# Two extra 512-column bf16 products in each step of three attentions, written into the PSUM ring's next bank

## The chip, the cores and the metric

The kernel runs on one core of one Trainium2 chip. The metric is the device time of one execution in microseconds (us). The kernel before was timed three times: 2797.93, 2802.47 and 2806.33 us, median 2802.47 us. The engines are called as in the profile: PE is TensorE (matrix products; PEld its weight loads), DVE VectorE, ACT ScalarE, POOL GpSimd, SP the engine that issues DMAs. PSUM is the memory that PE writes its products to, in eight banks of 512 fp32 columns.

## The reference

The program is four transformer layers on 256 tokens of width 1024, fp32 throughout. The first block has a gated MLP mixer and a differential attention, each followed by a squared-ReLU MLP and a gated input. The second block has two more attentions (`nsa_mixer`, `fox_mixer`), each followed by a mixture over 16384 small experts. Only the three attentions matter here. Cut to their cores:

```python
# differential attention: 8 heads, two score sets per head
sc = einsum('bqhcd,bkhcd->bhcqk', q, k) * scale            # causal, head dim 64
pr = softmax(sc);  attn = pr[:, :, 0] - lam * pr[:, :, 1]
o  = _rmsnorm(einsum('bhqk,bkhe->bqhe', attn, v), subln_g) * (1 - lambda_init)

# nsa: 16 heads, compressed keys plus two branches that here both see all causal keys
o = gate0 * (p_c @ v_cmp) + gate1 * (p_s @ v_slc) + gate2 * (p_w @ v_win)

# fox: 16 heads, scores with a running sum of forget gates
s = einsum('bhqd,bhkd->bhqk', q, k) + c[..., None] - c[:, :, None, :]
o = masked_softmax(s) @ v
```

## The kernel before

The 256 tokens are two tiles of 128 (tile 0, tile 1). Weights stream from HBM in blocks and each block is split into a high and a low float32r part (ACT makes the first, DVE the second); a product of two split numbers is three matmuls (`mm3`, lines 255 to 258). Four PSUM banks are the accumulators `A` (two per tile), the other four are a ring of scratch banks `B`: `ps` (line 260) takes the bank at the ring's front and puts it at the back. During an attention the ring is only two banks, since the other two hold the outputs.

An attention is written as a loop over units, one generator per tile (`unit(t)` in `diff_attention`, `nsa`, `fox`). A step of `attend` (line 899) issues up to seven parts, each of another unit, as a string says: `s` the scores (matmuls of 64 rows, 128 or 256 columns, then a bf16 mask product), `m` their row maxima on DVE, `e` the exponentials on ACT, `c` the scale, `t` the transposes on PE into a ring bank and the first part of their split on ACT, `l` the second part on DVE, `p` the products with v. With `"da": "t3l3c2p4e1s0m0"` a step turns the unit three back, and so on. A loop over n units has n plus the largest lag steps, so 12 steps per tile in the differential attention (da), 21 in nsa, 12 in fox; the last ones have no scores.

The order of the steps is a string too (`FILL`, read by `weave`): 0 and 1 are a step of tile 0's or tile 1's unit, c is a step of the product before the attention (six products of 512 columns), w one of the product after it. The program's order is the order on each engine's queue; nothing is rescheduled later. `identb` is a 128x128 bf16 identity, until now used only in the mask products (lines 1064, 1506, 1723).

```python
b = self.ring.pop(0)
self.ring.append(b)
```

Of the kernel before, what the change touches and what calls it, by code (L numbers as in the profile page):

```python
# [54 lines left out]
        "fox": "0cc0cc0c0c0c0111010101011010011w1w1w1w"}  # L55
ASIDE = {"go": "0234567", "wo": "0234567", "w10": "03", "w11": "", "nwo": "034567", "fwo": "0123457"}
# [3 lines left out]
def ffn_ops():  # L60
    """The pairs of up blocks ("u") and the down blocks ("d") in their order."""
    ops = [("u", 4)] + [("d", f) for f in range(4)] + [("u", 5)] + [("d", f) for f in range(4, 8)]
    for k in range(6, 14):
        ops += [("u", k), ("d", 2 * k - 4), ("d", 2 * k - 3)]
    return ops + [("u", 14), ("u", 15)] + [("d", f) for f in range(24, 32)]
# [5 lines left out]
class Stream:  # L71
    """The weights, block by block: a load, then the two float32r parts in a slot."""
# [9 lines left out]
    def aside(self, key):  # L82
        """True for the blocks whose second part GpSimd makes."""
        name, c = key[:-1], key[-1]
        while isinstance(name, tuple):
            name = "".join(str(x) for x in name) if not isinstance(name[0], tuple) else name[0]
        return str(c) in ASIDE.get(name, "")

# [3 lines left out]
    def open(self, pool, n):  # L92
        """n more slots, for the blocks that the plan lets use them."""
        self.free += [self._slot(pool, self.k.nm("x"), True) for _ in range(n)]
# [18 lines left out]
    def _one(self):  # L113
        """Splits the next block, if there is room for it."""
# [56 lines left out]
class Wide:  # L171
    """[128, 1024] in two banks of PSUM, of which one can be written while the other is read."""
# [15 lines left out]
class Build:  # L188
# [17 lines left out]
    def tick(self):  # L206
        """One step of each task."""
# [14 lines left out]
    def begin(self, task):  # L222
        """A task whose first step goes out at once."""
        next(task, None)
        return self.add(task)
# [4 lines left out]
    def need(self, t):  # L230
        """The input of a stage, tile t."""
# [28 lines left out]
    def ps(self, shape):  # L260
        """The next bank of the ring, as a shape."""
# [22 lines left out]
    def rstd(self, ms, eps, table=True, beside=None, r=None):  # L284
        """(ms + eps) ** -0.5, by ScalarE's table or, to leave its tables alone, by GpSimd; ms may be in two parts.

        beside() goes out while it is on its way."""
# [20 lines left out]
    def load_table(self, func):  # L308
        """ScalarE's table of func, ahead of its use."""
# [12 lines left out]
    def transpose_split(self, src, dst, c0, n, tsl, scale=None):  # L322
        """src [128 tokens, n*128]: chunks c0.. of dst[hi/lo][:, c, tsl]."""
# [8 lines left out]
    def wait(self, n):  # L332
        """Steps in which weights aren't split."""
# [5 lines left out]
    def turn_raw(self, t, xt, wait):  # L339
        """h's tile t, transposed and split into xt, without the norm's gain (the weights have it) and its r."""  # L340
# [6 lines left out]
    def turn_normed(self, t, g, xt, wait, table, part):  # L347
        """rmsnorm of h's tile t, transposed and split into xt; the last norm without xt."""
# [11 lines left out]
    def chain(self, t, m, post, pre, xt, wait=5, table=True):  # L360
        """h += m, or its rmsnorm; then the next stage's norm, with its gain pre or raw."""
# [25 lines left out]
    def block(self, key, c, x, t, out, ws, ncols, start, stop):  # L387
        """out[:, n] (tokens of tile t) += x^T w over row chunk c."""
# [13 lines left out]
    def ahead(self, keys, x, after=None, ncols=1024, start=True, stop=True):  # L402
        """Steps of a product for tile 0; those for tile 1 are put off."""
# [14 lines left out]
    def late(self):  # L418
        """The next block put off; False without one."""
# [18 lines left out]
    def linear(self, keys, x, after=None, ncols=1024, start=True, stop=True, lag=LAG, func=None):  # L438
        """A product for both tiles, tile 1 LAG blocks behind; after(t) once tile t is done.

        Towards the end tile 1 falls up to lag blocks behind, to be done beside what follows for tile 0, and func's
        table is loaded."""
# [13 lines left out]
    def lin_b(self, key, x, out):  # L456
        """out [n, tokens] of one block [128, 8, n]."""
# [134 lines left out]
    def open_side(self, n_gain):  # L592
        """What all but the expert layers use besides: a second input, slots of the stream, gains."""
# [7 lines left out]
    def dump(self, stage):  # L601
        """Ends the program after a stage, for tests of a part."""
# [42 lines left out]
    def load_x(self):  # L645
        """The input, the first weights before and between its tiles."""
# [4 lines left out]
    def load_p(self, i, also=None):  # L651
        """The layer's p, transposed, in two parts."""
# [8 lines left out]
    def proj(self, i, c, t, pt, ws):  # L661
        """pp = p w_proj, row chunk c of tile t."""
# [6 lines left out]
    def gmlp(self, xt, yt):  # L669
        nc, tc, a = self.nc, self.tc, self.a  # L670
        with tc.tile_pool(name="gm", bufs=1) as gp:
# [55 lines left out]
            def spatial():  # L727
                """s + b of all groups; u s of tile 0."""
# [46 lines left out]
    def ffn(self, i, xr, xt, also=None):  # L775
        """xr holds the raw input, xt will hold the normed one, xr the next stage's."""
# [72 lines left out]
    def scaled(self, x, t):  # L849
        """x = A[t] times the norm's r."""  # L850
# [3 lines left out]
    def inverse(self, t):  # L854
        """1 / r as a row."""
# [8 lines left out]
    def ple(self, i, xt, nxt):  # L864
# [11 lines left out]
        def mid(t, c):  # L876
            """The bias over r, that the sigmoid's scale takes back."""
# [21 lines left out]
    def attend(self, n, order, **parts):  # L899
        """Steps over n units: each one's parts trail one another, as far as order says.  # L900

        s: the scores; m: their maxima; e: the exponentials; c: the scale; t: the transposes and their first part;
        l: the second one; p: the product with v."""
        order = [(parts[k], int(b)) for k, b in zip(order[::2], order[1::2])]
        for i in range(n + max(b for _, b in order)):
            for f, b in order:
                if 0 <= i - b < n:
                    f(i - b)
            yield

    def weave(self, order, units, join, make):
        """The steps of both tiles' units (0, 1), those of tile 1's product before (c) and of tile 0's after (w).

        join(t) ends what tile t's units need, before the first of them or where order has z (0) or u (1); make begins
        the product after."""
# [39 lines left out]
    def maxima(self, s, n):  # L955
        """The negated row maxima of the score sets s [128, n, kn]."""
# [4 lines left out]
    def exps(self, s, n, kn, e, nm):  # L961
        """e = exp of the score sets s [128, n, kn] plus nm; the rows' sums."""
# [5 lines left out]
    def low(self, parts):  # L968
        """The second part of what the first was copied from."""
# [7 lines left out]
    def normed(self, e, r, kn, engine):  # L977
        """e [128, 2, kn] times r [128, 2]."""
# [17 lines left out]
    def diff_attention(self, xt, vx):  # L996
        """vx holds v and, after its use, nothing; xt becomes the input of w_o."""
        nc, tc, a = self.nc, self.tc, self.a
        H = 8
        with tc.tile_pool(name="da", bufs=1) as gp, tc.tile_pool(name="daw", bufs=2) as wp:  # L1000
# [48 lines left out]
            def unit(t):  # L1049
                """Steps of one component of two heads each."""  # L1050
# [25 lines left out]
                def scale(i):  # L1076
                    """e0 - lam (sum0 / sum1) e1; the rows' 1 / sum0 are left to fin."""
# [42 lines left out]
                return self.attend(H, ORDER["da"], s=scores, m=peak, e=soft, c=scale, t=turn, l=low, p=pv)  # L1120

            def fin(t, q, p3, norm):
                """The rmsnorm of four heads' norm p3."""
# [27 lines left out]
    def prep_rotary(self, pool):  # L1151
        """Steps to cos and sin of positions * inv_freq, [128, 2 tiles, 8], and lambda."""
# [62 lines left out]
    def rope64(self, dst, src, t, nh, wp, v=None):  # L1215
        """dst, src [128, nh, 64]; by VectorE or v."""
# [14 lines left out]
    def nsa(self):  # L1231
        """Tokens are fewer than the window and than the selected blocks: both branches see all keys."""
        nc, tc, a = self.nc, self.tc, self.a
        xt, qT = self.xb, self.xa
        with ExitStack() as ctx:
# [8 lines left out]
            # the compressed values of group g in rows 32j, at j, g; zeros in the other rows  # L1244
# [23 lines left out]
            def dup(x, fn, wait):  # L1268
                """x [128, 4, 2, 64] -> psum [128 = 2 copies of 64, 4, 128 tokens]; fn(p)."""
# [27 lines left out]
            def four(t):  # L1297
                """k and v of the compressed branch, k and v of the selected one."""
# [23 lines left out]
            def two(t):  # L1322
                """k and v of the window; the gates."""
# [14 lines left out]
            def build(kv):  # L1338
                """The blocks of tokens, with their places' embeddings."""
# [46 lines left out]
            def tail():  # L1386
                """The compressed keys and values."""
# [67 lines left out]
            def compressed(t):  # L1455
                """The compressed branch's weights of all heads, [128, 16, 32] with 16 used.

                Head (g, r) is at 8 (g // 2) + 4 (r // 2) + 2 (g % 2) + r % 2."""
# [32 lines left out]
            def unit(t):  # L1491
# [34 lines left out]
                def turn_compressed(a):  # L1526
                    """The weights of heads 8a.., turned."""
# [25 lines left out]
                def pv(i):  # L1553
# [7 lines left out]
                    def add(y, stop):  # L1561
                        """The compressed branch of a pair."""
# [19 lines left out]
                return self.attend(16, ORDER["nsa"], s=scores, m=peak, e=soft, c=scale, t=turn, l=low, p=pv)  # L1582
# [9 lines left out]
    def fox(self):  # L1592
# [3 lines left out]
        with ExitStack() as ctx:  # L1596
# [10 lines left out]
            # rows (1, 1, c_hi, c_lo) for queries and (-c_hi, -c_lo, 1, 1) for keys, of head 8a + 4v + 2u + w at  # L1607
            # 32 (2v + w), 2a + u: those that share a bank of scores are in the same rows
# [21 lines left out]
            def forget():  # L1630
                """c, the running sums of the forget gates' logarithms, into cx."""
# [73 lines left out]
            def unit(t):  # L1705
# [60 lines left out]
                return self.attend(8, ORDER["fox"], s=scores, m=peak, e=soft, c=scale, t=turn, l=low, p=pv)  # L1766
# [8 lines left out]
    def peer(self, li, side):  # L1775
        """All experts' products, times the gates (0 where an expert isn't chosen)."""
# [3 lines left out]
        with ExitStack() as ctx:  # L1780
# [20 lines left out]
            def select():  # L1801
                for t in range(NT):
# [24 lines left out]
                    # softmax over the 16 best  # L1827
# [15 lines left out]
                    # the entries of topi at the positions, by one-hot rows  # L1843
# [83 lines left out]
            def gbuild(half):  # L1927
                """H[half] *= G: the gates by expert (i, j) and token, from one-hot rows by selection."""
# [45 lines left out]
            def spread(bg, done, i, n, steps):  # L1974
                """bg's steps so far, after block i of n."""
# [40 lines left out]
            def weights(upto):  # L2016
                """The halves' rows, times the gates, in the input's place."""
# [37 lines left out]
def layout(inputs):  # L2055
    """The arrays of the program: the inputs laid out, and constants of the shapes."""
# [72 lines left out]
```

## Time and profile before

| what | value |
|---|---|
| median of three runs | 2802.47 us (2797.93 to 2806.33) |
| profiled execution, first to last instruction | 2807.0 us |
| PE busy | 2721.5 us, 97% |
| DVE, ACT, POOL busy | 2043.0, 1337.9, 141.0 us |
| mean granted TensorE clock | 0.964 of full |

The profiled execution is a run of its own. Its span, 2807.0 us, is already 0.7 us above the slowest of the timed runs, and what lies around the span is not in the profile. The page cuts the span into 40 slices of 70.2 us; the line PEclk gives the clock that was granted in each. A timeline row gives start, duration, engine, line and operation of one instruction; the difference of two starts is the pace. Matmuls overlap, so a pace is shorter than a duration.

### The profile page before, as it was taken

To read this page: it belongs to the slowest core of one execution; us is meant where nothing else is said; L and a number is where in the kernel's file an instruction comes from. 1 tells how busy PE (TensorE), PEld (TensorE's weight loads), DVE (VectorE), ACT (ScalarE), POOL (GpSimd) and SP (SyncE) were. 2 spreads that over 40 slices of the span, in tenths; PEclk is the share of its full clock that TensorE was granted. 3 is DMA by queue.
4 is the path that set the end of the run, shared out by engine and by line. 5 is a ranking of instruction groups with operands and counts; after the bars stand their busy time and mean duration, and the time that the engine had idled before them with its cause. 6 is when DMAs were issued, how large, how long until landed. Compare 5 with 4: busy or idle time off the path is not lost.

```text
span 2807.0 us, 44583 instructions
## 1 busy us (share of the span) xinstructions
PE 2721.5 (97%) x17590; PEld 2355.8 (84%) x17590; DVE 2043.0 (73%) x3492; ACT 1337.9 (48%) x2056; POOL 141.0 (5%) x130
## 2 busy tenths in 40 slices
PE   8999999999879999999999999999999999999998
PEld 6789777898657799999977788777899999877887
DVE  5655766656764579988899965455699888899664
ACT  5544654545443444444444454353554444444553
POOL 2200020000122100000000000010000000000000
PEclk9999997999986999999999999997999999999999
DMA  6655551554450146665555576440456655555663
GB/s 209 183 187 187 170 162 55 185 190 147 153 179 9 39 151 188 180 181 173 168 162 169 170 218 196 145 146 29 135 178 185 186 170 171 165 166 172 207 207 118
DMA packets 125237, 448.43 MB, mean 160 GB/s; under 512 B 15058, under 2 KB 15586, under 8 KB 125028
## 3 DMA queue, kind: packets, MB, share of 16 engines
q1 hardware_dynamic: 122404, 437.45, 50.7%
q0 software_dynamic: 2624, 8.14, 1.0%
q8 instruction: 137, 2.24, 0.3%
q14 instruction: 72, 0.59, 0.1%
HBM read 444.49 MB, written 1.05 MB: 159 GB/s over the span
## 4 chain that ended last, share of the span: by engine, by line
PE 32%; issue 31%; DVE 3%; ACT 1%; DMA 1%; POOL 0%; DVEq 0%; POOLq 0%; ACTq 0%
PE A L469 12%; PE B L256 4%; PE B L258 4%; PE B L257 4%; PE A L397 4%; PE B L1953 1%; DVE lob L249 1%; PE A L256 1%; PE A L1722 0%; PE B L1742 0%; PE A L257 0%; PE A L258 0%; PE B L1543 0%; PE A L1723 0%; DMA trir<-in_c_tri 0%
## 5 line engine op out<-in xcount | busy, mean ns | idle before, releaser
L248 ACT CAST hib<-raw 128x1024 fp32r<-128x1024 f32 x519 | 543.3, 1050 | 716.7 <-PE B L258 344.5
L249 DVE TENSOR_TENSOR lob<-raw,hib 128x1024 fp32r<-128x1024 f32 x508 | 618.5, 1220 | 189.9 <-ACT hib L248 189.3
L256 PE MATMUL B<-xa,hib 128*128 128x256 f32 x2096 | 593.1, 283 | 0.0
L257 PE MATMUL B<-xa,lob 128*128 128x256 f32 x2096 | 588.1, 281 | 0.1
L258 PE MATMUL B<-xa,hib 128*128 128x256 f32 x2096 | 587.2, 280 | 0.0
L469 PE MATMUL A<-hib,xa 128*128 128x512 f32 x1440 | 412.7, 400 | 4.9 <-ACT xa L248 4.9
L257 PEld LDWEIGHTS B<-xa,lob 128*128 128x128 f32 x2096 | 394.9, 188 | 1.2 <-DVE lob L249 0.6
L256 PEld LDWEIGHTS B<-xa,hib 128*128 128x128 f32 x2096 | 394.7, 188 | 0.0
L258 PEld LDWEIGHTS B<-xa,hib 128*128 128x128 f32 x2096 | 394.5, 188 | 0.0
L469 PEld LDWEIGHTS A<-hib,xa 128*128 128x128 f32 x1440 | 266.5, 189 | 65.8 <-ACT xa L248 5.2
L249 DVE TENSOR_TENSOR lox<-raw,hix 128x1024 fp32r<-128x1024 f32 x174 | 211.2, 1226 | 130.3 <-ACT hix L248 129.9
L248 ACT CAST hix<-raw 128x1024 fp32r<-128x1024 f32 x192 | 197.7, 1043 | 159.2 <-PE A L469 53.1
L469 PE MATMUL A<-lob,xa 128*128 128x512 f32 x720 | 227.4, 397 | 0.0
L1960 DVE SCALAR_TENSOR_TENSOR H<-B,H 128x512 f32<-128x512 f32 x128 | 169.6, 1328 | 1.0 <-PE B L1953 0.6
L397 PE MATMUL A<-hix,xb 128*128 128x512 f32 (+1 forms) x520 | 161.1, 409 | 4.9 <-DVE nv L252 4.2
L469 PEld LDWEIGHTS A<-lob,xa 128*128 128x128 f32 x720 | 135.6, 188 | 32.7
L469 PE MATMUL A<-hix,xa 128*128 128x512 f32 x480 | 133.3, 395 | 0.0
L252 DVE SCALAR_TENSOR_TENSOR lox<-raw,gcol,hix 128x1024 fp32r<-128x1024 f32 (+1 forms) x75 | 93.2, 1250 | 42.8 <-ACT hix L251 42.7
L397 PE MATMUL A<-hix,xa 128*128 128x512 f32 x400 | 121.3, 405 | 1.1 <-ACT hix L251 1.1
L397 PEld LDWEIGHTS A<-hix,xb 128*128 128x128 f32 x520 | 98.6, 198 | 26.0 <-DVE nv L252 4.8
L469 PEld LDWEIGHTS A<-hix,xa 128*128 128x128 f32 x480 | 90.0, 187 | 22.0
L249 DVE TENSOR_TENSOR xa<-H,xa 128x256 fp32r<-128x256 f32 x256 | 106.7, 420 | 0.9 <-ACT xa L248 0.9
(502 smaller groups left out, 4798.3 us busy)
## 6 DMA issues: line engine op xcount, KB each, us to landing
raw<-in_u SPq DMA_DIRECT2D x256, 512.0 KB, 3.6
raw<-in_v SPq DMA_DIRECT2D x256, 512.0 KB, 3.7
raw<-in_f_w_down SPq DMA_DIRECT2D x64, 512.0 KB, 3.5
raw<-in_w_up SPq DMA_DIRECT2D x48, 512.0 KB, 4.4
raw<-in_l_w_in SPq DMA_DIRECT2D x40, 512.0 KB, 3.6
raw<-in_b_w_qkv SPq DMA_DIRECT2D x24, 512.0 KB, 4.5
raw<-in_a_w_in SPq DMA_DIRECT2D x16, 512.0 KB, 4.2
raw<-in_f_w_up SPq DMA_DIRECT2D x16, 512.0 KB, 3.6
```

The costliest lines, as they stand in the source:

```text
L248: nc.scalar.copy(hi, src)
L249: engine.tensor_tensor(lo, src, hi.bitcast(F32), op=ALU.subtract)
L252: nc.vector.scalar_tensor_tensor(lo, src, scale, hi.bitcast(F32), op0=ALU.mult, op1=ALU.subtract)
L256: mm(out, s[0], m[0], start=start, stop=False)
L257: mm(out, s[1], m[0], start=False, stop=False)
L258: mm(out, s[0], m[1], start=False, stop=stop)
L397: self.nc.tensor.matmul(out[:, n0:n0 + n], xs[u], w[v][:, n0:n0 + n], start=start and i == 0, stop=stop and i == 2)
L469: self.nc.tensor.matmul(self.A[t][:, n0:n0 + 512], x[u][:, ts_], w[v][:, n0:n0 + 512], start=first and q == 0, stop=last and q == 2)
L1953: nc.tensor.matmul(p[:, t, :], A[:, t].rearrange("p a b -> p (a b)"), B[q][:, t].rearrange("p a b -> p (a b)"), start=q == 0, stop=q == 1)
L1960: nc.vector.scalar_tensor_tensor(hv, p, 1.0 / G_SCALE, hv, op0=ALU.mult, op1=ALU.mult)
```

## The change

`attend` gets a pair of numbers. Before the part `t` and before the part `s` of every step it now issues so many extra products: the bf16 identity times itself, read four times over, 512 columns, as a group of its own into the bank at the front of the ring, which is not taken out of the ring. All three attentions use (1, 1). The result is never read: whoever takes that bank next starts a new group in it. The extra products are issued also in steps where `t` or `s` have nothing to do. The diff also empties docstrings and comments, which makes no instruction.

```diff
+WARM = {"da": (1, 1), "nsa": (1, 1), "fox": (1, 1)}
...
+    def warm(self, n):
+        for _ in range(n):
+            p = self.ring[0].rearrange("p (a b) -> p a b", b=P)
+            self.nc.tensor.matmul(p, self.identb, self.identb[:, None, :].to_broadcast([P, 4, P]), start=True,
+                                  stop=True)
...
-    def attend(self, n, order, **parts):
+    def attend(self, n, order, warm=(0, 0), **parts):
-        order = [(parts[k], int(b)) for k, b in zip(order[::2], order[1::2])]
-        for i in range(n + max(b for _, b in order)):
-            for f, b in order:
+        before = dict(zip("ts", warm))
+        order = [(k, parts[k], int(b)) for k, b in zip(order[::2], order[1::2])]
+        for i in range(n + max(b for _, _, b in order)):
+            for k, f, b in order:
+                if k in before:
+                    self.warm(before[k])
                 if 0 <= i - b < n:
                     f(i - b)
             yield
...
-                return self.attend(H, ORDER["da"], s=scores, m=peak, e=soft, c=scale, t=turn, l=low, p=pv)
+                return self.attend(H, ORDER["da"], WARM["da"], s=scores, m=peak, e=soft, c=scale, t=turn, l=low, p=pv)
```

The calls in `nsa` and `fox` change in the same way. PE gets 180 more matmuls, each with a weight load: 48 in da, 84 in nsa, 48 in fox (two for each of 24, 42 and 24 steps). The other engines keep their rows. All line numbers after line 55 grow by 1, those after line 898 by 11.

PE at the start of the differential attention, before: `scr` is a tile of queries being turned into the two ring banks `B_71` and `B_72`, `qk` the keys and queries, `A_67` the bank of tile 0's scores, and the words in brackets are the engines whose counters the instruction waits for.

```order
L328 MATMUL B_71<-ident,scr_3024 128x128 x4
L328 MATMUL B_72<-ident,scr_3024 128x128 x4
L256 MATMUL A_67<-qk_2600,qk_2598 128x128 [waits DVE_49,PE_49]
L257 MATMUL A_67<-qk_2600,qk_2599 128x128
L258 MATMUL A_67<-qk_2601,qk_2598 128x128
L1064 LDWEIGHTS identb
L1064 MATMUL A_67<-maskb,identb 128x128
```

The same place after:

```order
L329 MATMUL B_71<-ident,scr_3024 128x128 x4
L329 MATMUL B_72<-ident,scr_3024 128x128 x4
L904 LDWEIGHTS identb
L904 MATMUL B_71<-identb 128x512 [waits DVE_49]
L904 LDWEIGHTS identb
L904 MATMUL B_71<-identb 128x512
L257 MATMUL A_67<-qk_2600,qk_2598 128x128 [waits PE_49]
L258 MATMUL A_67<-qk_2600,qk_2599 128x128
L259 MATMUL A_67<-qk_2601,qk_2598 128x128
```

Two products of 512 columns stand between the last transposes and the first scores, and the first of them waits for DVE, which has to have read `B_71`.

PE in nsa, where a step of tile 0 (scores in `A_68`, the exponentials `e` turned into the ring) is followed by one of tile 1 (scores in `A_70`), before:

```order
L1506 MATMUL A_68<-maskb,identb 128x128
L1543 MATMUL B_72<-ident,e_6513 128x128 [waits Pool_49]
L1543 MATMUL B_72<-ident,e_6513 128x128
L256 MATMUL A_70<-nkT_5575,xa_84 128x256
L257 MATMUL A_70<-nkT_5575,xa_85 128x256
L258 MATMUL A_70<-nkT_5576,xa_84 128x256
```

The same place after:

```order
L1517 MATMUL A_68<-maskb,identb 128x128
L904 LDWEIGHTS identb
L904 MATMUL B_72<-identb 128x512
L1554 MATMUL B_72<-ident,e_6566 128x128 [waits Pool_49]
L1554 MATMUL B_72<-ident,e_6566 128x128
L904 LDWEIGHTS identb
L904 MATMUL B_71<-identb 128x512 [waits DVE_49]
L257 MATMUL A_70<-nkT_5623,xa_84 128x256
L258 MATMUL A_70<-nkT_5623,xa_85 128x256
L259 MATMUL A_70<-nkT_5624,xa_84 128x256
```

Each step has one extra product ahead of its scores and one ahead of its transposes. The one ahead of tile 1's scores waits until DVE has read the bank that the turn before this one had filled. Of the 180 extra products 47 wait for DVE in this way (5 in da, 30 in nsa, 12 in fox).

## Rows read from the trace of the kernel before

**Rows 1.** The page: busy time of the engines, and the clock in 40 slices

```profile
PE 2721.5 (97%) x17590; PEld 2355.8 (84%) x17590; DVE 2043.0 (73%) x3492; ACT 1337.9 (48%) x2056; POOL 141.0 (5%) x130
...
PEclk9999997999986999999999999997999999999999
```

**Rows 2.** Stretches: us, busy of PE, PEld, DVE, ACT, POOL; clock, DMA

```profile
415.00:456.00 41.00, 37.38 (x153) 30.70 (x153) 23.90 (x65) 15.24 (x55) 7.05 (x5) 0.50 0.09 26
829.00:859.00 30.00, 25.60 (x118) 22.17 (x118) 21.50 (x45) 9.65 (x28) 9.96 (x9) 0.54 0.24 85
859.00:903.00 44.00, 42.89 (x189) 34.64 (x188) 18.67 (x59) 17.88 (x71) 10.10 (x13) 0.58 0.00 1
903.00:950.00 47.00, 43.96 (x309) 36.51 (x308) 26.56 (x71) 25.25 (x83) 14.51 (x16) 1.00 0.00 1
1903.00:1941.00 38.00, 38.00 (x142) 28.98 (x142) 18.83 (x43) 13.81 (x51) 2.35 (x1) 0.51 0.04 15
```

**Rows 3.** Waits of PE in da, 391 to 462 us

```profile
PE B L257 <- DVE at L971: 2.1, 1, 2.1
PE B L328 <- DVE scr L1133: 1.5, 1, 1.5
```

**Rows 4.** Waits of PE in nsa, 829 to 951 us

```profile
PE B L328 <- DVE scr L1229: 3.4, 1, 3.4
PE A L256 <- ACT e L965: 3.2, 3, 1.2
```

**Rows 5.** Waits of PE in fox, 1876 to 1952 us

```profile
PE B L1742 <- DVE pt L971: 0.6, 1, 0.6
PE B L1742 <- DVE e L981: 0.5, 1, 0.5
PE A L256 <- DVE fv L252: 0.5, 1, 0.5
```

**Rows 6.** Timeline of PE in da: 512-column products, then 256-column scores

```profile
389.46 1.07 PE L397 MATMUL A<-hix,xb 128*128 128x512 f32 x4
390.36 0.62 PE L397 MATMUL A<-lox,xb 128*128 128x512 f32 x2
...
408.97 1.91 PE L397 MATMUL A<-hix,xb 128*128 128x512 f32 x4
410.68 1.05 PE L397 MATMUL A<-lox,xb 128*128 128x512 f32 x2
...
413.53 0.38 PE L256 MATMUL A<-qk,qk 64*128 64x256 f32 x1 [1.34 <-DVE xa L252]
...
414.24 0.38 PE L256 MATMUL A<-qk,qk 64*128 64x256 f32 x1
...
422.07 0.58 PE L256 MATMUL A<-qk,qk 64*128 64x256 f32 x1
...
423.23 0.58 PE L256 MATMUL A<-qk,qk 64*128 64x256 f32 x1
```

**Rows 7.** Stretch, mask products alone (line 1064, da): PE, PEld busy, clock, DMA

```profile
384.00:415.00 31.00, 3.20 (x14) 1.34 (x14) 0.94 0.46 150
```

**Rows 8.** The same, line 1506, nsa

```profile
829.00:859.00 30.00, 3.69 (x14) 1.40 (x14) 0.54 0.24 85
859.00:903.00 44.00, 7.40 (x27) 2.73 (x27) 0.58 0.00 1
```

**Rows 9.** The same, line 1723, fox

```profile
1876.00:1903.00 27.00, 3.22 (x14) 1.34 (x14) 0.94 0.44 139
```

**Rows 10.** Timeline, da's start: first scores (PE), second split of both ring banks (DVE)

```profile
392.24 0.32 PE L256 MATMUL A<-qk,qk 64*128 64x128 f32 x1
...
392.53 1.29 DVE L249 TENSOR_TENSOR qk<-B,qk 128x512 fp32r<-128x512 f32 x2 [0.51 <-ACT qk L248]
```

**Rows 11.** Timeline in nsa: transposes of tile 1 (PE), their second split (DVE)

```profile
913.78 0.61 PE L1543 MATMUL B<-ident,e 128*128 128x128 f32 x4
...
916.02 0.69 DVE L971 TENSOR_TENSOR pt<-B,pt 128x512 fp32r<-128x512 f32 x1 [1.07 <-ACT pt L974]
```

More of the change, by code (lines that the diff above doesn't have):

```diff
@@ L1580, in pv @@
                         self.split(y[0], y[1], p[r].rearrange("p (o x) s -> p o x s", o=2))
-                return self.attend(16, ORDER["nsa"], s=scores, m=peak, e=soft, c=scale, t=turn, l=low, p=pv)
+                return self.attend(16, ORDER["nsa"], WARM["nsa"], s=scores, m=peak, e=soft, c=scale, t=turn, l=low, p=pv)
             def after(t):
@@ L1764, in pv @@
                         self.split(oT[0][r, gs, ts_], oT[1][r, gs, ts_], p[r, :, 128 * b:128 * b + 128])
-                return self.attend(8, ORDER["fox"], s=scores, m=peak, e=soft, c=scale, t=turn, l=low, p=pv)
+                return self.attend(8, ORDER["fox"], WARM["fox"], s=scores, m=peak, e=soft, c=scale, t=turn, l=low, p=pv)
             def after(t):
```

## The prediction

> **What bounds the kernel now.** I read the page first. PE is busy for 97% of the span [rows 1], so a change on another engine would hardly show, and anything added to PE shows unless it falls into a wait. The line PEclk is the exception to an even picture: 9 nearly everywhere, but lower in the slices in which the three attentions lie (slices 7, 12, 13 and 28, with 7, 8, 6 and 7 tenths). I then cut the attentions into stretches [rows 2]. The reader is to see two things. In da from 415 to 456 us, in fox from 1903 to 1941 us and in most of nsa up to 903 us the clock is at 0.50, the lower of its two levels (1.2 and 2.4 GHz); 0.54 and 0.58 are mixtures. And PE is still the engine that sets the pace: 37.38 of 41, 42.89 of 44 and 38.00 of 38 us busy, while DVE has 23.90, 18.67 and 18.83. From 903 to 950 us nsa's steps run at 1.00, PE 43.96 of 47. So the bound in these stretches is PE at half clock.
>
> The waits of PE confirm it: 3.6 us in the two largest of da [rows 3], 6.6 us in nsa [rows 4], 1.6 us in all of fox [rows 5]. Last I took prices from the timeline [rows 6]. Four 512-column products take 390.36 - 389.46 = 0.90 us at 2.4 GHz, 0.23 each, and 410.68 - 408.97 = 1.71 us at 1.2 GHz, 0.43 each. One head's scores of 256 columns take 414.24 - 413.53 = 0.71 us at 2.4 and 423.23 - 422.07 = 1.16 us at 1.2, so work that is moved to the upper level saves (1.16 - 0.71) / 1.16, about 0.4 of its time. By columns alone it could be 0.5; I take 0.4, as these scores are most of the work there.
>
> **What the change adds.** 180 products on PE, none on any other engine and no DMA, SP's and POOL's queues stay as they are. Their price by rows is 0.23 us or 0.43 us each, and it depends on the clock; they are bf16 with a weight load of their own, while the priced rows are float32r, whose loads are longer, so a little less than 0.23 is possible and nothing above 0.43 is likely apart from waits. If all 180 ran at 2.4 GHz they would cost 41 us, at 1.2 GHz 77 us. What they can bring is the clock. The lower level is there for 41 us in da, (1 - 0.54) / 0.5 x 30 = 28 and (1 - 0.58) / 0.5 x 44 = 37 us in nsa, 37 us in fox, 143 us together; at 0.4 that is 57 us at most. So the best case and the cost are of one size, and the sum is made stage by stage.
>
> What the engine did before the clock fell and rose decides how much of it is got back. In da, while steps of tile 0 alternate with steps of the product before it (six 512-column products between two steps), the clock is 0.94 on average [rows 7], and fox's first stretch has the same 0.94 [rows 9]; both fall when only attention steps of 64-row scores are left, and with PE busy without a break. Two such wide products in each step are a third of what these alternating stretches have. I therefore expect the clock to hold longer where the steps are PE's own work already, and not to hold where nsa's tile 0 starts: there PE is busy for only 25.60 of 30 us, with DVE at 21.50 [rows 2].
>
> - **da.** Until 415 us 14 mask products, so 7 steps [rows 7], 14 extra products at 0.23: +3.2. From 415 us I let 30 of the 41 us go to 2.4 GHz: -12. The other 34 products, 26 at 0.23 and 8 at 0.43: +9.4. Products that stand in front of the waits of 2.1 and 1.5 us fill part of them: -2. Sum -1.4.
> - **nsa.** 829 to 859 us stays at 1.2 GHz: 14 products (14 mask products, two to a step) [rows 8], 6.0, of which 3 lie in the waits for DVE and ACT [rows 4]: +3. 859 to 903 us: two thirds of 37 us, 25 us, go to 2.4 GHz, -10; 27 products, 18 at 0.23 and 9 at 0.43, +8. The last 84 - 14 - 27 = 43 products stand in a stretch that has the full clock already and can only pay: 43 x 0.23 = 9.9, less 2 in ACT's waits, +7.9. Sum +8.9.
> - **fox.** 14 products before 1903 us [rows 9]: +3.2. Half of the 37 us goes to 2.4 GHz: -7.4. 34 products, 22 at 0.23 and 12 at 0.43: +10.3. Almost no wait covers them [rows 5]. Sum +6.1.
> - **New waits.** 47 products wait for DVE's reading of their bank. At da's start the first scores began at 392.24 us, while DVE splits the two banks from 392.53 for 1.29 us, so the first bank is free near 393.2: 1.0 us, and the scores and the product steps queued behind on PE wait with it [rows 10]. fox starts in the same way: 2 us for both. In nsa the second split of a bank starts 2.2 us after its transposes [rows 11], and a wide product that comes two turns later has mostly that long to wait for nothing. No row shows such a wait; it lies between 0, if a step always passes first, and 0.8 us (a split that ends 2.4 us after its transposes less one 128-column step) for each. I take 2 us for the 42 others, near the lower end, since PE's present waits for these splits are few. Sum +4.
>
> Together -1.4 + 8.9 + 6.1 + 4 = +18 us. The profiled execution's span of 2807.0 us becomes 2825; it lies 4.5 us above the median of the timed runs, and since that is the scatter of one kernel (2797.93 to 2806.33) I add the 18 us to the median: 2820 us.
>
> The rest of the program is to stay. After each attention PE is the bound again, so what the attention loses or gains is not taken back: the DMA share in the stretches is 0.00 to 0.24 [rows 2], the weights are already there.
>
> One rule speaks against any gain here. The row first: in fox PE waits 1.6 us in all, in pieces of 0.6 us and less, from 1876 to 1952 us [rows 5], and the clock is at 0.51 for 38 us with PE busy throughout [rows 2]. The Trainium skill, "TensorE: Matmul & The Clock Gate", section "Why this matters for your kernels", says that what makes the clock drop is an idle gap between bursts of matmuls. By that rule products which fill no gap change no clock, and the sum would be that of the second rival below, +56 us. The trace does not agree: here the clock fell without a gap.
>
> **The rivals.**
> - *All of it is held (faster).* The products keep the clock at 2.4 GHz from the first step of each attention on. For it: nsa's own steps have 1.00 from 903 us on [rows 2], and the alternating stretches hold. Against it: 829 to 859 us, where PE waits. Time: -57 + 41 - 7 (in waits) + 4 = -19 us, 2784. It decides if nsa's tile 0 holds the clock from its start.
> - *The clock is where it was (slower).* The products change no level. For it: the rule above, and that a step at 1.2 GHz gets longer by 0.86 us as well as denser. Against it: the rows of fox. About 90 products at 0.43 and 90 at 0.23, 39 + 21 - 7 + 4 = +56 us, 2859. It decides from the point that da's stretch after 415 us stays at 0.50.
> - *The two sides cancel (no change).* da as forecast, fox held throughout (-14.8 + 48 x 0.23 = -3.8) and nsa held from 859 us on (3 - 14.8 + 6.2 + 7.9 = +2.3), waits +4: +1 us, 2804.
> - *The bank is the bound (slower).* Each of the 47 waiting products waits 0.8 us, as PE at 2.4 GHz runs ahead of ACT and DVE: 18 - 4 + 38 = +52 us, 2854. For it: 2.4 us from transposes to the end of the split [rows 11]. Against it: two banks alternate, so most have a whole step in between.
>
> **How the numbers follow.** Forecast 0.50, cancelled 0.19, all held 0.13, clock as before 0.10, bank 0.08. The likeliest's own range is 2806 to 2836 us: a third more or less of the clock's return of 29 us, and new waits between 0 and 10 us. The range of 8 in 10 takes in the cancelled case and most of the two ends: 2786 to 2852 us. What a measurement here can tell from no change is about 0.3%, 8.4 us. Slower: nearly nine tenths of the forecast, the two slow rivals and a tenth of the cancelled case, 0.64. Faster: all held and a little of the cancelled case, 0.16. The same: 0.20.
>
> **What will show it.** In the changed trace 180 matmuls at line 904 with a pace of 0.2 to 0.43 us; the clock in da between 415 and 445 us mostly at 1.00; in nsa about 0.5 until the two tiles alternate, then mostly 1.00; in fox a mixture. PE's waits for DVE at line 904 should add to a few us, with one near 1 us at the start of da and of fox. The forecast is wrong if da stays at 0.50 (then the second rival), if nsa is at 1.00 from its first steps (then the first), or if line 904 waits for DVE for more than 15 us in all.

## The result, and the profile after

The changed kernel takes 2826.61 us (median of 15 runs, 2810.34 to 2838.45), the kernel before 2802.13 us in the 15 runs beside it (2792.77 to 2810.84). The ratio is 1.0084 [1.0067 to 1.0101]: slower by 24.5 us, where 18 were forecast. The profiled execution, 2837.45 us with a span of 2835.7 us, lies at the slow end of these runs; its mean granted clock is 0.969, and the runs of this kernel have 0.969 to 0.981, the highest clock with 2812.62 us. So a trace of one run and the median differ here by 11 us.

The page of the kernel after, its first part and the clock in 40 slices, which answer to [rows 1]:

```profile
PE 2749.5 (97%) x17770; PEld 2357.4 (83%) x17770; DVE 2038.4 (72%) x3492; ACT 1338.6 (47%) x2056; POOL 141.6 (5%) x130
...
PEclk9999999999887999999999999997999999999999
```

180 more matmuls, and the 7 of da's slice is gone. By stretches (columns as in [rows 2]), the kernel after:

```profile
415.00:440.00 25.00, 22.83 (x145) 16.24 (x145) 17.82 (x52) 12.44 (x47) 4.71 (x4) 1.00 0.14 43
440.00:451.00 11.00, 9.90 (x37) 8.24 (x37) 6.58 (x17) 2.79 (x7) 1.01 (x1) 0.53 0.00 0
829.00:891.00 62.00, 56.88 (x212) 40.82 (x211) 27.61 (x72) 16.17 (x66) 14.42 (x17) 0.50 0.10 35
891.00:950.00 59.00, 53.84 (x338) 41.54 (x338) 27.53 (x77) 26.54 (x94) 15.76 (x18) 0.94 0.00 1
1885.00:1921.00 36.00, 34.29 (x167) 24.22 (x165) 17.35 (x28) 19.35 (x42) 15.29 (x7) 0.95 0.40 130
1921.00:1953.00 32.00, 32.00 (x112) 21.89 (x112) 11.99 (x28) 9.45 (x36) 1.36 (x1) 0.52 0.05 17
```

In this run da holds 2.4 GHz for 25 us more, as forecast (the lower level that begins at 415 us [rows 2] lasted 44 us and is now 10 long). nsa is at 1.2 GHz through 891 us, so the clock that was to come back there did not, and its full stretch is no longer full (0.94 for 1.00). In fox the lower level starts at 1921 us for 1903, of which 13 us are the shift of all that comes before, and is 31 us long for 38; but shorter spells behind it make up for that. Summed over each attention, the time at 1.2 GHz is 48 us before and 14 after in da, 72 and 75 in nsa, 44 and 44 in fox: in this run only da gained clock. The same instructions of DVE in both traces, subtracted, give what each attention costs: da -3.4 us (forecast -1.4), nsa +22 (forecast +8.9), fox +13.8 (forecast +6.1). By the stretches of [rows 2], nsa costs +3.5 us for the steps that were at 829 to 859 us, +6.0 for those at 859 to 903 and +14.0 for those at 903 to 950, where the forecast had +3, -2 and +7.9; its steps before 829 us gain the 1 us that is left. Line 904 is the line of the extra products; durations in ns (least, median, greatest), then the idle time before them (the matmuls wait for DVE; the entry `issue` is of the weight loads, PEld):

```profile
L904 PEld LDWEIGHTS <-identb x180: 95/98/152, 388.1 to 1980.9; 128*128 128x128 bf16 x180
L904 PE MATMUL B<-identb x180: 376/379/650, 389.3 to 1980.9; 128*128 128x512 bf16 x180
its engine sat idle before it (us, times) until:
  issue: 10.5, 18
  DVE pt L982: 5.2, 5
  DVE at L982: 2.9, 1
  DVE cT L250: 2.2, 4
  DVE xa L253: 1.7, 1
  DVE qk L250: 1.0, 1
```

The waits for DVE add to 13.0 us where the forecast had 4. Not all of that is new, since other lines wait less: all waits of PE for other engines in the three attentions (pauses above 0.15 us) add to 25.7 us after and 21.2 before.

### The profile page after: what moved, and what is told of

Its sections match the earlier page's. It is cut to its first block, busy times and chain, and to the rows that moved or that the text cites. A ratio compares the mean times of both kernels' runs of the same rounds, so it can differ in the third digit from the quotient of the medians.

```text
span 2835.7 us, 44921 instructions
## 1 busy us (share of the span) xinstructions
PE 2749.5 (97%) x17770; PEld 2357.4 (83%) x17770; DVE 2038.4 (72%) x3492; ACT 1338.6 (47%) x2056; POOL 141.6 (5%) x130
## 4 chain that ended last, share of the span: by engine, by line
PE 32%; issue 30%; DVE 4%; ACT 1%; DMA 1%; POOL 0%; DVEq 0%; ACTq 0%; POOLq 0%
PE A L470 12%; PE B L257 4%; PE B L259 4%; PE B L258 4%; PE A L398 4%; PE B L1964 1%; DVE lob L250 1%; PE B L904 1%; PE A L257 1%; PE A L1733 0%; PE A L259 0%; PE A L258 0%; PE B L1753 0%; PE A L1734 0%; DMA trir<-in_c_tri 0%
```

## The experiments

**One attention at a time.** The products are kept in one attention and left out of the two others.

```diff
-WARM = {"da": (1, 1), "nsa": (1, 1), "fox": (1, 1)}
+WARM = {"da": (1, 1), "nsa": (0, 0), "fox": (0, 0)}
```

> The 48 products of the differential attention alone, none in nsa and fox. Theory (products pay their columns, the clock gives back where it is held): -3 us, between -7 and 0, granted clock near 1.00 in the stage until the steps without scores; nsa and fox as before. Rival (the waits for the ring's bank carry the loss): the stage has one long wait of 2.9 us and 1 us at its start, so +4 us.

> The 84 products of nsa alone. Theory: +15 to +22 us, most of the whole loss, since the clock stays at 0.50 while the products stand in its first 60 us, and the last 40 have a full clock already. Rival (waits): nsa's waits at line 904 were 4 us, so +4 to +6 us.

> The 48 products of fox alone. Theory: +5 to +14 us, the clock held longer than before but falling again for about 30 us. Rival (waits): its waits at line 904 were 5 us, so +5 us and no more.

| products in | median, us | before, us | ratio |
|---|---|---|---|
| da | 2802.76 | 2800.83 | 1.0006 [0.9987 to 1.0025] |
| nsa | 2817.41 | 2800.83 | 1.0053 [1.0033 to 1.0073] |
| fox | 2809.77 | 2800.83 | 1.0035 [1.0019 to 1.0050] |

The three differences, 1.9, 16.6 and 8.9 us, add to 27.4 us beside the change's 24.5: the attentions are nearly independent, and nsa pays most. For nsa and fox the time lies where the theory had it, and nsa's is not the rival's +4 to +6. For da the interval, -4 to +7 us, holds both the theory's -3 and the rival's +4. What da gains is not there in each execution. Its runs go from 2790.81 to 2819.09 us, and the profiled one, at 2814, did not hold the clock at all:

```profile
415.00:456.00 41.00, 41.00 (x153) 28.54 (x153) 18.35 (x52) 13.30 (x49) 6.77 (x4) 0.53 0.08 26
```

**Thirty-two columns instead of 512.** All 180 products stay where they are, with 32 columns each.

```diff
-            p = self.ring[0].rearrange("p (a b) -> p a b", b=P)
-            self.nc.tensor.matmul(p, self.identb, self.identb[:, None, :].to_broadcast([P, 4, P]), start=True,
-                                  stop=True)
+            self.nc.tensor.matmul(self.ring[0][:, :32], self.identb, self.identb[:, :32], start=True, stop=True)
```

> All 180 products, with 32 columns in place of 512: same places, same bank, same weight load, same waits, hardly any columns. Theory: clock as before, waits of some 5 us and 180 x 0.05 us of weight loads, +5 to +12 us. Rival (waits and weight loads carry the loss): +20 us or more, as with 512 columns.

Measured: 2824.56 us, ratio 1.0084 [1.0064 to 1.0105], the change's own. The rival stood and the theory did not. So the columns, which were the main cost of the forecast, are not what the kernel loses once the clock is counted. The mean granted clock of its runs is 0.962, against 0.965 for before and 0.974 for the change: columns cost time and bring clock, and the two come out even. What stays when the columns go is the waits, 13.6 us for DVE, and 180 products with their weight loads. The view of the products' line in this kernel:

```profile
L903 PE MATMUL B<-identb x180: 176/189/250, 390.1 to 1974.1; 128*128 128x32 bf16 x180
its engine sat idle before it (us, times) until:
  issue: 10.9, 19
  DVE pt L980: 7.2, 7
  DVE at L980: 1.9, 1
  DVE cT L250: 1.8, 3
  DVE xa L253: 1.7, 1
  DVE qk L250: 1.0, 1
```

**Twice as many.** Two products in place of each one, 360 in all.

```diff
-WARM = {"da": (1, 1), "nsa": (1, 1), "fox": (1, 1)}
+WARM = {"da": (2, 2), "nsa": (2, 2), "fox": (2, 2)}
```

> Two products where the change has one, 360 in all, at the same places in the ring's bank. Theory: no new waits (the second product follows the first in a bank that it has), 180 x 0.23 us = 41 us of columns at 2.4 GHz less a better clock (0.980 or more instead of 0.9745, worth 13 us or more): +40 to +60 us against before, so 16 to 36 more than the change. Rival (columns are free and only the waits and loads of the first cost): within 12 us of the change, +24 to +36.

Measured: 2836.87 us, ratio 1.0125 [1.0103 to 1.0147], 34.8 us over before and 10 over the change, where the rival stood. The second 180 products cost 10 us, 0.06 each, but with a mean clock of 0.983 for 0.974. At 21 us for each 0.01 (the runs of the change) that clock is worth 17 us or more, so their columns cost some 28 us, about 0.15 each: an estimate. In its trace da and fox are held, nsa's middle mostly; its stretches, for [rows 2]:

```profile
415.00:456.00 41.00, 38.61 (x227) 26.62 (x227) 24.70 (x68) 15.47 (x55) 5.98 (x5) 0.96 0.08 26
859.00:903.00 44.00, 42.66 (x222) 27.55 (x219) 17.61 (x57) 16.56 (x70) 9.11 (x13) 0.84 0.00 1
1903.00:1941.00 38.00, 38.00 (x194) 24.73 (x192) 18.21 (x34) 17.81 (x51) 14.27 (x6) 1.00 0.30 97
```

The second product of a pair finds the bank free: with 360 products the matmuls' waits for DVE at this line add to 10.4 us, no more than with 180. The run does not say what the first one pays; the next four do.

**The bank, by itself.** Both products of a step now stand before the scores, only in steps that have scores (128 in all): once in the ring's next bank, once in the bank that these scores are about to fill, for which they have to wait anyway.

In the ring:

```diff
-                if k in before:
-                    self.warm(before[k])
                 if 0 <= i - b < n:
+                    if k == "s":
+                        self.warm(warm, self.ring[0])
```

In the scores' bank:

```diff
-                if k in before:
-                    self.warm(before[k])
                 if 0 <= i - b < n:
+                    if k == "s":
+                        self.warm(warm, self.A[tile_n].halves[(i - b) % 2])
```

> Two products of 512 columns ahead of the scores and none ahead of the transposes, in steps that have scores only: 128 products into the ring's front bank. It is the control of the next kernel. Theory now (a loss of three parts: columns, weight loads with their issue, and waits for the bank, less what the clock gives back): +10 to +20 us, about 8 to 10 us of it waits at line 904 for DVE, granted clock 0.970 to 0.975 as a mean over the runs. Rival (columns against clock alone, no part for waits): the same time as the next kernel.

> The same 128 products at the same places, written into the bank that the scores behind them are about to start anew, so that they wait for what the scores wait for anyway and for nothing of the ring. Theory: 7 to 11 us less than the kernel with the ring's bank, so 0 to +12 us against before, waits at line 904 for DVE under 2 us. Rival (waits cost nothing, they only move): within 3 us of the ring's kernel.

The same two with 32 columns:

```diff
-            p = bank.rearrange("p (a b) -> p a b", b=P)
-            self.nc.tensor.matmul(p, self.identb, self.identb[:, None, :].to_broadcast([P, 4, P]), start=True,
+            p = bank[:, :32]
+            self.nc.tensor.matmul(p, self.identb, self.identb[:, :32], start=True,
```

> The 128 products go before the scores into the bank that these scores then fill, as in the run with the score bank, but 32 columns wide instead of 512. Theory (the loss with 32 columns in the ring came from the waits for the bank and the falls of the clock behind them, in nsa's stretch from 904 to 930 us above all): without these waits narrow products cost little, 2799 to 2808 us; nsa loses 5 us at most from 904 to 930 us (10 with 32 columns in the ring), and the waits for DVE at the products' line stay under 3 us in all. The clock is as before or a little lower (0.960 to 0.967), since 32 columns bring nothing. Rival (each product costs by its own weight load and by the pause that it makes between matmuls, whatever its columns and its bank): 128/180 of the 22 us that 180 narrow products in the ring took, 2816 us or more, with nsa's loss from 904 to 930 us near 7 us.

> The fourth of a square: 128 products before the scores, 32 columns wide, in the ring's next bank. It differs from the run with 32 columns in the score bank (ratio 1.0002) by the bank alone, and from the run with 512 columns before the scores in the ring (1.0055) by the width alone. Theory (the bank decides, and 512 columns pay for themselves by the clock): 2812 to 2820 us, a ratio of 1.004 to 1.007; waits for DVE at the products' line of 8 us or more; nsa loses 7 us or more from 904 to 930 us; clock at 0.960 to 0.964. Rival (what cost 22 us with 180 narrow products was their number and the ones before the transposes and in the last steps, which are gone here, and not the bank): 2806 us or less, nsa's loss from 904 to 930 us under 4 us.

| 128 products | ring's next bank | the scores' own bank |
|---|---|---|
| 512 columns | 2817.26 us, 1.0055 [1.0034 to 1.0076], clock 0.973 | 2804.75 us, 1.0015 [1.0000 to 1.0030], clock 0.976 |
| 32 columns | 2819.83 us, 1.0049 [1.0032 to 1.0065], clock 0.964 | 2800.57 us, 1.0002 [0.9990 to 1.0014], clock 0.966 |

Down a column, sixteen times the width changes the ratio by 0.0006 and 0.0013, 2 to 4 us. Along a row, the bank changes it by 0.0040 and 0.0047, 11 to 13 us. So among these four the bank decides, and the products' number and weight loads do not: 128 narrow products in the scores' bank cost nothing that can be measured. All four times lie where the theories had them. The bank does not explain the whole 24.5 us of the change, though: 128 products in the ring lose 15 us over the kernel before, with either width. The other 9 us went with the 52 products of the steps without scores, which are left out, and with 64 that moved from ahead of the transposes to ahead of the scores; no run separates these two. The products' waits for DVE are 9.2 us (512 columns) and 8.6 us (32) in the ring, 1.8 us in the scores' bank with either width; there 3.8 and 3.5 us of waits for ACT stand at this line, in front of scores that need the same bank.

How the bank comes to cost that much is seen in nsa where both tiles run and the kernel before has the full clock. The rows are the stretch between the same two row maxima of DVE (columns as in [rows 2]). In the kernel before (the runs with da or fox alone, which have no products here, take 25.3 us each):

```profile
904.20:929.60 25.40, 25.35 (x184) 21.05 (x183) 16.22 (x47) 15.91 (x56) 9.31 (x11) 1.00 0.00 1
```

In the change itself:

```profile
907.60:944.40 36.80, 34.00 (x208) 26.52 (x207) 16.71 (x48) 16.04 (x56) 9.32 (x11) 0.91 0.00 1
```

With 512 columns in the ring:

```profile
906.10:940.80 34.70, 31.26 (x202) 23.86 (x201) 16.64 (x47) 15.91 (x56) 9.30 (x11) 0.95 0.00 1
```

With 32 columns in the ring:

```profile
895.70:931.10 35.40, 32.02 (x202) 27.81 (x201) 16.61 (x47) 15.94 (x56) 9.32 (x11) 0.81 0.00 1
```

With 512 columns in the scores' bank:

```profile
892.10:921.50 29.40, 29.16 (x202) 22.40 (x201) 16.68 (x48) 15.91 (x56) 9.30 (x11) 1.00 0.01 1
```

With 32 columns in the scores' bank:

```profile
891.10:917.00 25.90, 25.80 (x202) 22.40 (x201) 16.25 (x47) 15.94 (x56) 9.31 (x11) 1.00 0.01 2
```

The last four have 18 products here (202 matmuls for 184). In the scores' bank they take 0.5 us with 32 columns and 4.0 with 512, 0.19 us for each product's added width. In the ring they take 9 to 10 us, and PE is idle for 3.4 of them (34.70 - 31.26, 35.40 - 32.02). The clock there is 0.95 and 0.81. With 32 columns that is (1 - 0.81) / 0.5 x 35.4 = 13.5 us at 1.2 GHz, of which 0.4 is lost time, 5.4; with the idle time that is 8.8 of the 9.5 us that the bank costs here (35.40 - 25.90). With 512 columns the bank costs 5.3 us (34.70 - 29.40): the same idle time, and 1.4 us for the 3.5 us at 1.2 GHz. A wait followed by a fall, in the timeline of the ring with 32 columns (start, us, engine, line):

```profile
904.91 0.28 PE L259 MATMUL B<-pt,nv 128*128 128x256 f32 x1
906.09 0.20 PE L904 MATMUL B<-identb 128*128 128x32 bf16 x2 [0.90 <-DVE cT L250]
906.22 0.38 PE L257 MATMUL A<-nkT,xa 64*128 64x256 f32 x1
...
911.09 0.58 PE L257 MATMUL A<-nkT,xa 64*128 64x256 f32 x1
```

A first score matmul of 0.38 us right after the wait is 0.58 us five microseconds on, in a place that ran at 2.4 GHz before. That the wait makes the clock fall is read from the order of the two, and it does not follow every wait. In this trace the waits of 0.90 and 1.44 us (at 906 and 924 us) have a fall within 1.5 us behind them, and one of 0.81 us (at 898 us) has none. With 512 columns in the ring a wait of 1.44 us at 934 us has none, and in the kernel before a wait for ACT of 1.16 us at 931 us has none. So the bank's cost is shown by exchanging the bank; that its part in the clock comes from the waits is not shown.

**Only where the clock falls.** The scores' bank, and only in steps whose neighbours in `FILL` are attention steps too: 92 products of 512 columns.

```diff
+        for j, k in enumerate(order):
+            self.hot = not set(order[max(j - 1, 0):j + 2]) & set("cw")
...
+                    if k == "s" and self.hot:
```

> Products into the score bank, two ahead of the scores, only in steps whose neighbours in the order's string are attention steps too (no step of a product before or after, and not the tail behind the string): 92 products. Theory: 92 x 0.2 us = 18 us of cost, hardly any waits, and about the clock of the change (0.970 to 0.975, worth 12 to 22 us): -5 to +5 us against before. Rival (the places don't matter): cost and return both in proportion to 92 of 180, +12 us.

Measured: 2800.12 us (2790.47 to 2816.26), ratio 1.0003 [0.9986 to 1.0020], clock 0.974. The clock is that of the change and the loss is gone, but nothing is left over: its runs reach 2790.47 us where the clock is 0.980 and 2816.26 where it is 0.968. No version here beats the kernel before.

## Why the prediction was right, and where it was not

- **Direction and the forecast case: right.** PE at half clock is the bound, the products cost PE time, and the clock gives back a part. All three parts are seen: the columns' price (0.19 us at 2.4 GHz for 480 columns, beside 0.23 taken for 512 from [rows 6]), the clock's return, the waits. The sum is near, but its parts are not: nsa and fox cost more than twice their forecast in the profiled run, and alone 16.6 and 8.9 us by the medians.
- **da: right in the profiled run** (-3.4 us for -1.4; the lower level 13.7 us long in all instead of 47.8), but its hold varies from run to run, which the forecast did not have; alone, da comes out at no change.
- **New waits: a mis-sized term.** The forecast had +4, of which 2 for 42 waits near the lower of its bounds (0 and 0.8 us each; without the two starts 45 of the 47 are left), "since PE's present waits for these splits are few" [rows 3 to 5]. That reason was wrong. In the order of before, a whole set of scores stands between the turn that fills a bank and the next one that takes it; the extra product asks ahead of these scores. The waits measured 13.0 us, in 12 pieces and not in 47. da's first one, priced at 1.0 us from [rows 10], measured 1.0; fox's, taken to be alike, 1.7. The bound of 0.8 was passed by five others, 0.9 to 2.9 us. The longest, in da, is not new: before, PE waits 2.1 us for the same tile of DVE [rows 3], and with the scores' bank 2.9 us, both at the products with v. Waits at other lines fell by 8.5 us, where 7 were taken off in the stages, so that PE's waits rose by 4.5 us in all where the forecast's terms give -3.
- **A lower clock where it had been full was no term at all.** In nsa's full-clock stretch the forecast had columns only (43 products, +7.9 for the whole of it). The 25 us of it that are shown above lost 11.4 us in the change, 9 to 10 with 18 ring products, and 4.0 with 512 columns in the scores' bank; the clock there is 0.91, 0.95 and 0.81, and 1.00.
- **The clock's return in nsa: wrong, and in fox not seen.** In nsa two thirds of the lower level from 859 to 903 us were to go to 2.4 GHz, -10 us; the profiled run had 0.50 through 891 us. The trace with nsa alone shows the same 61 us at 1.2 GHz from 831 us on. For fox's -7.4 us the traces show nothing: the time at 1.2 GHz in it is 44 us with products (the change, and fox alone), and 44, 34 and 27 us without (before, da alone, nsa alone). With both products before the scores the lower level ends earlier (51 us long in the ring, 38 in the scores' bank, one profile each). Whether the place of the products or the execution decides that is open.
- **The total.** Runs of the change differ by 24.8 us between clocks of 0.969 and 0.981, 21 us for each 0.01. The mean clock rose from 0.965 to 0.974, so some 20 us came back where 29 were forecast, and without them the products cost about 44 us where 47 were: an estimate from these runs. Of the 44 the waits at the products are 13 instead of 4, so all else is 31 instead of 43. So errors of -12 us (columns), +9 (waits) and +9 (clock) cancel in part: that the sum came this near is partly luck.
- **The rivals.** All held is excluded by nsa's stretch. Clock as before is excluded by the runs, 0.969 to 0.981 for a mean of 0.965 before; by da's stretch alone it would not be, since the run with da alone stayed at 0.53. The two sides do not cancel, since the interval of the ratio begins at 1.0067. The bank as the bound had the right place and too high a price (38 us for 13.0). In da the clock of the change's profiled run falls where PE waits 2.9 us: 1.00 from 438 to 440 us, 0.72 in the next us, 0.50 behind. The Trainium skill, "TensorE: Matmul & The Clock Gate", section "Why this matters for your kernels", has that idle gaps between bursts of matmuls make the clock drop: da's fall agrees. The gaps that it means are longer than the waits of nsa's stretch above, 0.2 to 1.4 us, so for these the section says nothing. I had set the rule aside as a whole because fox falls without a gap [rows 2, 5]. For da my reading, a fall "with PE busy without a break", was wrong: in [rows 6] a wait of 1.34 us ends at 413.53 us, and the stretch at 0.50 begins at 415 us.

## What to carry to other kernels

A filler product is to be priced by the buffer that it writes and by what it holds up in the queue, before its columns: let it write where the next instruction has to wait anyway. Where the clock is the bound, a wait may cost a second time in the clock behind it (some waits here did, as far as the order of events tells), so look at the granted clock after each new wait. And where the clock's level differs between executions, take the gain from the median of many runs; one trace with the clock held is not a gain.

## What the hardware showed unexpectedly

- 180 products with a sixteenth of the columns took the same time as wide ones (1.0084 both), at a lower granted clock (0.962 for 0.974).
- One and the same kernel gets another mean clock in each execution: 0.969 to 0.981 for the change, 0.963 to 0.974 with products in da alone, and the time goes with it (correlation -0.96 in the latter's 12 runs).
